# Short convolution of a hybrid decoder layer: taps on overlapping pieces of the product in PSUM, half of the tokens as one split tile with a halo, Silu in half 0

## Chip, cores and metric

The kernel runs on one core of a Trainium2 chip. The metric is the device time of one execution in microseconds (us). A core has TensorE (PE; its weight loads are listed as PEld), VectorE (DVE), ScalarE (ACT), GpSimd (POOL), and SyncE (SP), which issues the DMAs here.

## The reference, cut to what matters

One inference step of a two-layer decoder trunk, for a prompt of 2048 tokens and for a sample group of 8 single tokens with a cache of 2048 positions each. Layer 0 is a pooling mixer beside differential attention. Layer 1 is a gated DeltaNet beside a spatial-gating MLP. The change touches the front of layer 1, where the q, k and v channels (2304 of them) pass a causal convolution of four taps along the tokens and a Silu:

```python
qkv, u_sg, v_sg, b, a, gate = split_cols(h @ w_in, (CONV_CH, SG_W, SG_W, DELTA_HEADS, DELTA_HEADS, MIX_W))
ext = jnp.concatenate([conv_prefix.astype(qkv.dtype), qkv], axis=1)
conv = sum(ext[:, j:j + L] * conv_w[j] for j in range(CONV_WIDTH))       # CONV_WIDTH = 4
q, k, v = split_cols(jax.nn.silu(conv), (DELTA_W, DELTA_W, DELTA_W))     # DELTA_W = 768
q = l2norm(q.reshape(B, L, DELTA_HEADS, DELTA_DK)) * (DELTA_DK ** -0.5)
k = l2norm(k.reshape(B, L, DELTA_HEADS, DELTA_DK))
...
o, s_new = gated_delta_rule(q, k, v, beta, logg, s0)
...
return mixed @ w_out, ext[:, -(CONV_WIDTH - 1):], s_new, vv.reshape(B, L, SG_W)
```

The last three rows of `ext` are an output, `new_conv_prompt`.

## The kernel before

All products are done in three passes: each operand is split into a high and a low part of the type F32R (`hi`, `lo`), and `mm3` (lines 184 to 186) issues hi x hi, hi x lo and lo x hi into one PSUM bank. `fm_block` runs this over the eight slices of the 1024 model channels, 24 matmuls with 128 output channels on the partitions and the tokens as columns.

The stages follow one another: `in_even`, `attention`, `out_even` (layer 0's output product, the norm of layer 1 and the transposed, split tokens), then `odd` (layer 1). `odd` handles the 2048 tokens as two halves of 1024. The split tokens of a half lie in three pairs of tiles, of 512, 256 and 256 columns (`QSUB`), made by `h_subs` and `big_pair`. `out_even` fills those of half 0; the tokens of half 1 wait in DRAM (`hb`), and `load_half` loads and splits them when half 1 begins, with the 8 sample tokens as extra columns of the last pair.

For each half `odd` goes through 18 blocks of 128 convolution channels (`conv_silu`), with `gated_v` (the MLP's v part) and `decay` before block 14, and then through the spatial part and the gate blocks. In `conv_silu` each of the three subtiles gives one PSUM bank (`bank("acc")`, three banks in turn, tags X twice and D). ScalarE copies it into `raw` (line 1211), an SBUF tile with four columns ahead for the tokens before (`chalo`, lines 1206 and 1217). When a block's 1024 columns are in `raw`, two pieces of 512 follow: ScalarE multiplies by the first tap (line 1225), VectorE adds the other three in place (line 1227), ScalarE takes Tanh of half of it (line 1229), and VectorE makes (tanh + 1) * x (line 1230), which is twice the Silu; the constants of the delta stage (`delta_blocks`) take this factor into account. `store` writes the result to DRAM (`y1`), from where the delta stage reads it. `cx` and `cth` come from four buffers of 512 columns (`t512`).

Side work is interleaved by `tick`. In half 0 this is `sample_values`: for 8 sample rows, 16 pages of the value cache each are loaded by SP (line 531, three buffers `kp`), multiplied by GpSimd (line 626), added by VectorE (line 628), and summed over the partitions by TensorE (line 634). A page load is placed on SP behind the last `store` traced before it (`issue_after(self.mark)`). In half 1 it is the chunked delta rule of half 0 (`delta`), with a higher priority. The gate function `silu2_store` uses the same Tanh form (lines 418 and 420), with the second input read from PSUM. Weights are loaded and split one unit ahead (`w_unit`, lines 162 to 165).

The order of each engine's instructions is fixed when the kernel is built: a planner takes the traced order, the priorities and simulated ready times (`schedule_with_timeline_sim=True`). Each engine then runs its list in order.

Of the kernel before, what the change touches and what calls it, by code (L numbers as in the profile page):

```python
# [10 lines left out]
F32 = mybir.dt.float32  # L11
F32R = mybir.dt.float32r
BF16 = mybir.dt.bfloat16
I32 = mybir.dt.int32
AF = mybir.ActivationFunctionType
ALU = mybir.AluOpType
# [4 lines left out]
P = 128  # L21
D = 1024
NT = 2048
NS = 8
# [7 lines left out]
KT = 8  # L32
SUB = ((0, 384), (384, 384), (768, 256))
QSUB = ((0, 512), (512, 256), (768, 256))


# [25 lines left out]
class Net:  # L62
# [842 lines left out]
    def out_even(self):  # L905
        nc, I = self.nc, self.I
        st = ExitStack()
        self.bigs, self.t5 = {"b": 1, "s": 2}, T5
        self.banks = dict(acc="XXDA", h="Y", side="C")
        self.wp = self.pool(self.oddst, "wp", 2)  # L910
        self.wbufs = 2, 2, 1
        self.hp = hp = self.pool(self.oddst, "hp", 3)
        self.big = self.pool(self.oddst, "big", 1)
        wk = self.pool(st, "wk", 2, side="right")
# [7 lines left out]
        self.sides["values"] = self.sample_values()  # L922
        self.subs = self.h_subs(0, 0)
        for n, t in enumerate(P3):
# [9 lines left out]
            self.tick(VA if n < 8 else VB, "values")  # L934
        st.close()


    def odd_consts(self, st):
# [41 lines left out]
        nc.sync.dma_start(self.bmask, I["bmask"])  # L980
        self.chalo = t("chalo", [P, 18, 4])
        nc.gpsimd.memset(self.chalo, 0.0)
        self.S = [t(f"S{g}", [P, 3, P]) for g in range(2)]
# [73 lines left out]
    def odd(self):  # L1057
# [12 lines left out]
        for half in range(2):  # L1070
# [11 lines left out]
            for cb in range(18):  # L1082
                if cb == CB:
                    ba = self.gated_v(half, subs, wk, hp)
                    gt = self.decay(half, ba, wk)
                self.conv_silu(half, cb, subs, nxt(), wk, hp)
            if half == 0:
# [25 lines left out]
        self.tick(10000, "sample")  # L1113
        tiles = [self.big_pair(i, w) for i, (_, w) in enumerate(QSUB)]
        self.sides["w_out"] = self.w_out(I["w_out_o"], tiles, lambda: hp.tile([P, 4 + HALF], F32, tag="hx", name="wraw"), W2)
# [28 lines left out]
    def load_half(self, hp, wk):  # L1144

        nc = self.nc
        subs = self.h_subs(1, NS)
        for t in range(8):
            raw = hp.tile([P, 4 + HALF], F32, tag="hx", name="hk")[:, :D]
            nc.sync.dma_start(raw, self.hb[t])  # L1150
            raw = raw.rearrange("p (k t) -> p k t", t=P)
            hi, lo = self.tok_tile(subs, t)
            nc.scalar.copy(hi, raw)
            (nc.gpsimd if t % 3 == 2 else nc.vector).tensor_tensor(lo, raw, hi.bitcast(F32), ALU.subtract)
        hi, lo = (a[:, :, 256:] for a in subs[2][:2])
        nc.vector.tensor_copy(hi, self.hs)
        nc.vector.tensor_tensor(lo, self.hs, hi.bitcast(F32), ALU.subtract)
        return subs
# [42 lines left out]

    def conv_silu(self, half, cb, subs, unit, wk, hp):

        nc, O = self.nc, self.O
        raw = hp.tile([P, 4 + HALF], F32, tag="hx", name="raw")
        nc.vector.tensor_copy(raw[:, 0:4], self.chalo[:, cb, :])
        for hi, lo, t0, n, ns in subs:
            ps = self.bank("acc", 512)
            self.fm_block(ps[:, :n + ns], unit, (hi, lo))
            o = 4 + t0 - half * HALF  # L1210
            nc.scalar.copy(raw[:, o:o + n], ps[:, :n])  # L1211
            if ns:
                nc.vector.tensor_copy(self.raws[:, cb, :, 3], ps[:, n:n + ns])
            self.tick(self.pace)
            self.tick(2 if n == 512 else 1, "values")
        if half == 0:
            nc.vector.tensor_copy(self.chalo[:, cb, :], raw[:, HALF:HALF + 4])
        else:
            nc.sync.dma_start(O["new_conv_prompt"][cb * P:cb * P + P, :], raw[:, HALF + 1:HALF + 4],
                              allow_slow_non_contiguous=True)  # L1220
        w = self.convw[:, cb, :]
        for q in range(2):
            o = 1 + q * 512
            x = self.t512(wk, "cx")
            nc.scalar.mul(x, raw[:, o:o + 512], w[:, 0:1])  # L1225
            for j in range(1, 4):
                nc.vector.scalar_tensor_tensor(x, raw[:, o + j:o + j + 512], w[:, j:j + 1], x, ALU.mult, ALU.add)  # L1227
            th = self.t512(wk, "cth")
            nc.scalar.activation(th, x, AF.Tanh, scale=0.5)
            nc.vector.scalar_tensor_tensor(th, th, 1.0, x, ALU.add, ALU.mult)  # L1230
            c0 = half * HALF + q * 512
            self.store(self.y1[cb * P:cb * P + P, c0:c0 + 512], th)

# [113 lines left out]
    def delta_blocks(self, y, gt, dl):  # L1347
# [8 lines left out]
        s, c = (dl.tile([P, NH], F32, tag=nm, name=nm, bufs=3) for nm in ("ks", "kc"))  # L1356
        nc.vector.tensor_scalar(s, ss, 4 * EPS, 0.5, ALU.add, ALU.mult)
        self.rstd(ss, 4 * EPS)
        nc.vector.tensor_tensor(s, s, ss, ALU.mult)
        nc.vector.tensor_tensor(c, ss, ss, ALU.mult)  # L1360
        nc.vector.tensor_tensor(c, c, gt[0][:, y["t"], :], ALU.mult)

        nc.vector.tensor_scalar(qe, qe, P * EPS, 4 * P * EPS * EPS, ALU.mult, ALU.add)
        self.de(1).tensor_tensor(N, N, c[:, :, None].broadcast_to([P, NH, P]), ALU.mult)
# [395 lines left out]
```

## Time and profile before

| | |
|---|---|
| median of 3 runs | 3147.14 us (3144.58 to 3152.71) |
| the profiled execution | 3144.06 us |
| its span, first to last instruction | 3142.4 us |
| mean granted clock of TensorE | 0.958 of full speed |
| busy share of the span | PE 89%, PEld 80%, DVE 69%, ACT 48%, POOL 54% |

A busy share is the part of the span in which an engine had an instruction of the program running. Matmuls overlap in the records, so the work of TensorE is better read from the distance of their starts. A group of instructions is given by line, engine, operation, out<-in, shapes and count, then busy us, mean ns of one, and the idle time of the engine just before them with what ended it. L1227 is line 1227 of the kernel.

### The profile page before, as it was taken

Reading aid. Unit: us, or ns where it says so; the run is one execution under the profiler, and the core shown is the slowest. Engines: PE = TensorE matmul, PEld = TensorE weight load, DVE = VectorE, ACT = ScalarE, POOL = GpSimd, SP = SyncE. Lnnn points to the kernel's source line nnn. Section 1 sums busy time; section 2 is a strip of 40 time slices with the busy share of each in tenths; the row PEclk is TensorE's granted clock in tenths of the full one; section 3 lists DMA queues with packets and bytes.
Section 4 is the critical chain, followed back from the end, with each engine's and each line's share of the span. In section 5 each row is a group of like instructions: output and inputs, shape, how many; then the busy total and the mean of one; then the engine's idle time right before and its main releaser. Section 6 shows DMA issues by size and latency. Waiting matters only on the chain. (4 is left out here: it accounts for less than half of the span.)

```text
span 3142.4 us, 57680 instructions
## 1 busy us (share of the span) xinstructions
PE 2812.4 (89%) x20425; PEld 2515.9 (80%) x20425; DVE 2170.1 (69%) x4012; ACT 1516.3 (48%) x4464; POOL 1688.4 (54%) x1220
## 2 busy tenths in 40 slices
PE   8999899989998899989888778999899988878999
PEld 7999799889777777778777667888788877767887
DVE  5465456464998899876669998658788575457562
ACT  6643245534877787752222223445554533344331
POOL 4566545571667776664665655455544244255541
PEclk9999899999999999999998889999999999979999
DMA  4567766556244423237765554435333233467543
GB/s 164 167 192 254 240 219 202 190 166 183 70 102 118 121 60 84 71 101 221 245 217 180 164 164 160 130 103 154 86 95 100 82 99 112 121 159 212 164 119 98
DMA packets 423149, 462.55 MB, mean 147 GB/s; under 512 B 84683, under 2 KB 324212, under 8 KB 422860
## 3 DMA queue, kind: packets, MB, share of 16 engines
q1 hardware_dynamic: 422860, 458.86, 49.5%
q8 instruction: 162, 2.65, 0.4%
q14 instruction: 127, 1.04, 0.1%
HBM read 332.41 MB, written 126.33 MB: 146 GB/s over the span
## 5 line engine op out<-in xcount | busy, mean ns | idle before, releaser
L184 PE MATMUL acc<-sh,whi 128*128 128x256 f32 (+2 forms) x1328 | 392.5, 296 | 7.4 <-ACT raw L1211 4.8
L186 PE MATMUL acc<-sh,wlo 128*128 128x256 f32 (+2 forms) x1328 | 389.6, 294 | 1.5 <-DVE wlo L165 1.2
L185 PE MATMUL acc<-sl,whi 128*128 128x256 f32 (+2 forms) x1328 | 389.6, 293 | 0.0
L184 PE MATMUL acc<-bh,whi 128*128 128x512 f32 (+2 forms) x904 | 347.4, 384 | 23.9 <-ACT raw L1211 11.2
L186 PE MATMUL acc<-bh,wlo 128*128 128x512 f32 (+2 forms) x904 | 348.5, 386 | 6.6 <-DVE wlo L165 4.1
L185 PE MATMUL acc<-bl,whi 128*128 128x512 f32 (+2 forms) x904 | 346.3, 383 | 1.9 <-DVE bl L873 1.9
L813 ACT ACTIVATE p<-sc,nb 128x512 f32<-128x512 f32 (+3 forms) x480 | 302.3, 642 | 74.0 <-DVE nb L812 63.1
L836 POOL TENSOR_TENSOR p<-p,cf 128x512 f32<-128x512 f32 (+3 forms) x240 | 236.8, 1005 | 182.4 <-DVE cf L832 46.0
L626 POOL TENSOR_TENSOR kp<-kp,at 128x768 f32<-128x768 f32 x120 | 210.9, 1766 | 171.1 <-DMA kp<-in_cache_v 151.9
L165 POOL TENSOR_TENSOR wlo<-wraw,whi 128x1024 fp32r<-128x1024 f32 (+1 forms) x90 | 221.3, 2463 | 127.4 <-ACT whi L163 127.2
L812 DVE TENSOR_REDUCE nb<-sc 128x1 f32<-128x512 f32 (+3 forms) x480 | 276.0, 598 | 17.5 <-PE sc L809 9.1
L184 PEld LDWEIGHTS acc<-sh,whi 128*128 128x128 f32 (+1 forms) x1328 | 260.3, 196 | 17.5 <-ACT raw L1211 6.0
L548 POOL TENSOR_TENSOR kp<-kp,qb 128x768 f32<-128x768 f32 x88 | 168.9, 1925 | 183.6 <-DMA kp<-in_cache_k 133.8
L185 PEld LDWEIGHTS acc<-sl,whi 128*128 128x128 f32 (+1 forms) x1328 | 260.5, 196 | 6.5 <-issue 2.8
L186 PEld LDWEIGHTS acc<-sh,wlo 128*128 128x128 f32 (+1 forms) x1328 | 259.9, 196 | 4.7 <-issue 1.5
L184 PE MATMUL acc<-whi,bh 128*128 128x256 f32 x864 | 249.6, 289 | 0.3 <-DVE th L416 0.3
L185 PE MATMUL acc<-wlo,bh 128*128 128x256 f32 x864 | 248.3, 288 | 0.5 <-POOL wlo L165 0.5
L186 PE MATMUL acc<-whi,bl 128*128 128x256 f32 x864 | 248.4, 288 | 0.0
L1227 DVE SCALAR_TENSOR_TENSOR cx<-raw,convw,cx 128x512 f32<-128x512 f32 x216 | 230.9, 1069 | 11.2 <-ACT cx L1225 8.7
L850 PE MATMUL pv<-v,pt 128*128 128x128 f32 x1632 | 218.7, 282 | 15.9 <-ACT pt L848 9.1
L808 PE MATMUL sc<-kh,q 128*128 128x512 f32 (+2 forms) x480 | 210.5, 439 | 24.4 <-ACT p L813 20.9
L850 PEld LDWEIGHTS pv<-v,pt 128*128 128x128 f32 x1632 | 202.2, 195 | 30.5 <-ACT junk L853 13.8
(443 smaller groups left out, 8344.6 us busy)
## 6 DMA issues: line engine op xcount, KB each, us to landing
kp<-in_cache_k SPq DMA_DIRECT2D x128, 384.0 KB
kp<-in_cache_v SPq DMA_DIRECT2D x128, 384.0 KB
wraw<-in_w_in_e SPq DMA_DIRECT2D x56, 512.0 KB
wraw<-in_w_in_o SPq DMA_DIRECT2D x56, 512.0 KB
mc<-cat SPq DMA_DIRECT2D x72, 256.0 KB
mg<-sg SPq DMA_DIRECT2D x72, 256.0 KB
y<-cth SPq DMA_DIRECT2D x72, 256.0 KB
kh<-kh SPq DMA_DIRECT2D x48, 256.0 KB
```

Source lines behind the costliest of these rows:

```text
L165: e.tensor_tensor(lo, raw, hi.bitcast(F32), ALU.subtract)
L184: mm(out, ah, bh, start=first, stop=False)
L185: mm(out, ah, bl, start=False, stop=False)
L186: mm(out, al, bh, start=False, stop=last)
L548: (nc.vector if j % 3 == 2 else nc.gpsimd).tensor_tensor(k, k, qb, ALU.mult)
L626: nc.gpsimd.tensor_tensor(h3(w), h3(v), self.at[:, b, j, :, None].broadcast_to([P, NH, P]), ALU.mult)
L808: mm(sc[:, :w], qc, kh[:, c, :w], start=True, stop=False)
L812: nc.vector.tensor_reduce(nb[:, c, j:j + 1], sc[:, :n], AX.X, ALU.max, negate=True)
L813: nc.scalar.activation(p[:, c, :n], sc[:, :n], AF.Exp, bias=nb[:, c, j:j + 1], accum_out=l[:, c, j:j + 1])
L836: nc.gpsimd.tensor_tensor(p[:, 1, :n], p[:, 1, :n], cf[:, 1, j:j + 1].broadcast_to([P, n]), ALU.mult)
L850: mm(pv, tt[:, t, :], kvt[j][2][:, t, :], start=j == 0 and t == 0, stop=j * 4 + t == nk - 1)
L1227: nc.vector.scalar_tensor_tensor(x, raw[:, o + j:o + j + 512], w[:, j:j + 1], x, ALU.mult, ALU.add)
```

## The change

All tokens of a half, with four columns ahead of them for the last tokens of the half before and eight behind for the sample tokens, lie in one pair of split tiles (`hh`, `hl`). The convolution's product is taken in three pieces of 342, 342 and 340 output tokens (`CSUB`), each with the four columns ahead of it, so that neighbouring pieces overlap and every tap of a piece reads its PSUM bank directly. `raw` and `chalo` are gone. Half 0 uses ScalarE's Silu; half 1 keeps Tanh, with the taps halved beforehand (`convh`). The result is the Silu itself and not its double, so the delta stage's constants lose their factor. The last conv rows are collected in `clast` and written by one DMA. The other users of the subtiles get slices of the new pair (`odd_subs`).

```diff
+CSUB = ((0, 342), (342, 342), (684, 340))
+HW = 4 + HALF + NS
...
     def out_even(self):
-        self.big = self.pool(self.oddst, "big", 1)
+        big = self.pool(self.oddst, "big", 1)
+        self.hh, self.hl = (big.tile([P, KT, HW], F32R, name=nm) for nm in ("bh", "bl"))
+        for a in (self.hh, self.hl):
+            nc.gpsimd.memset(a[:, :, 0:4].bitcast(F32), 0.0)
...
-        self.subs = self.h_subs(0, 0)
+        self.subs = self.odd_subs(0, 0)
...
+    def odd_subs(self, half, ns):
+        return [(*(a[:, :, 4 + t0:4 + t0 + n + (ns if t0 == 768 else 0)] for a in (self.hh, self.hl)),
+                 half * HALF + t0, n, ns if t0 == 768 else 0) for t0, n in QSUB]
...
     def odd_consts(self, st):
-        self.chalo = t("chalo", [P, 18, 4])
-        nc.gpsimd.memset(self.chalo, 0.0)
+        self.clast = t("clast", [P, 18, 3])
+        self.convh = t("convh", [P, 18, 4])
+        nc.vector.tensor_scalar(self.convh, self.convw, 0.5, None, ALU.mult)
...
     def odd(self):
-                self.conv_silu(half, cb, subs, nxt(), wk, hp)
+                self.conv_silu(half, cb, nxt(), wk)
+            if half:
+                nc.sync.dma_start(O["new_conv_prompt"].rearrange("(k p) j -> p k j", p=P), self.clast,
+                                  allow_slow_non_contiguous=True)
...
-        tiles = [self.big_pair(i, w) for i, (_, w) in enumerate(QSUB)]
+        tiles = [tuple(a[:, :, c0:c0 + w] for a in (self.hh, self.hl)) for c0, w in QSUB]
...
     def load_half(self, hp, wk):
-        subs = self.h_subs(1, NS)
+        subs = self.odd_subs(1, NS)
+        for a in (self.hh, self.hl):
+            nc.gpsimd.tensor_copy(a[:, :, 0:4], a[:, :, HALF:HALF + 4].bitcast(F32))
...
-    def conv_silu(self, half, cb, subs, unit, wk, hp):
-        nc, O = self.nc, self.O
-        raw = hp.tile([P, 4 + HALF], F32, tag="hx", name="raw")
-        nc.vector.tensor_copy(raw[:, 0:4], self.chalo[:, cb, :])
-        for hi, lo, t0, n, ns in subs:
+    def conv_silu(self, half, cb, unit, wk):
+        nc = self.nc
+        w = (self.convw, self.convh)[half][:, cb, :]
+        for a, n in CSUB:
+            ns = NS if half and a + n == HALF else 0
+            m = n + 4 + ns
             ps = self.bank("acc", 512)
-            self.fm_block(ps[:, :n + ns], unit, (hi, lo))
-            o = 4 + t0 - half * HALF
-            nc.scalar.copy(raw[:, o:o + n], ps[:, :n])
+            self.fm_block(ps[:, :m], unit, tuple(h[:, :, a:a + m] for h in (self.hh, self.hl)))
+            x = self.t512(wk, "cx")[:, :n]
+            nc.scalar.mul(x, ps[:, 1:1 + n], w[:, 0:1])
+            for j in range(1, 4):
+                nc.vector.scalar_tensor_tensor(x, ps[:, 1 + j:1 + j + n], w[:, j:j + 1], x, ALU.mult, ALU.add)
             if ns:
-                nc.vector.tensor_copy(self.raws[:, cb, :, 3], ps[:, n:n + ns])
+                nc.vector.tensor_copy(self.raws[:, cb, :, 3], ps[:, n + 4:m])
+                nc.vector.tensor_copy(self.clast[:, cb, :], ps[:, n + 1:n + 4])
+            if half == 0:
+                th = x
+                nc.scalar.activation(th, x, AF.Silu)
+            else:
+                th = self.t512(wk, "cth")[:, :n]
+                nc.scalar.activation(th, x, AF.Tanh)
+                nc.vector.scalar_tensor_tensor(th, th, 1.0, x, ALU.add, ALU.mult)
+            self.store(self.y1[cb * P:cb * P + P, half * HALF + a:half * HALF + a + n], th)
             self.tick(self.pace)
-            self.tick(2 if n == 512 else 1, "values")
...
+            self.tick(1 if a else 2, "values")
...
     def delta_blocks(self, y, gt, dl):
-        nc.vector.tensor_scalar(s, ss, 4 * EPS, 0.5, ALU.add, ALU.mult)
-        self.rstd(ss, 4 * EPS)
+        nc.vector.tensor_scalar(s, ss, EPS, None, ALU.add)
+        self.rstd(ss)
...
-        nc.vector.tensor_scalar(qe, qe, P * EPS, 4 * P * EPS * EPS, ALU.mult, ALU.add)
+        nc.vector.tensor_scalar(qe, qe, P * EPS, P * EPS * EPS, ALU.mult, ALU.add)
```

In the diff of `conv_silu`, the removed tail (halo, the output DMA and the loop over two pieces of 512) is left out; it stands in the function above.

## Rows read from the trace of the kernel before

**Rows 1.** The page: busy tenths of PE and DVE in 40 equal slices.
```profile
PE   8999899989998899989888778999899988878999
DVE  5465456464998899876669998658788575457562
```

**Rows 2.** Windows by stage: busy (count) of PE, PEld, DVE, ACT, POOL; PEclk, DMA.
```profile
1400.00:1640.00 240.00, 215.52 (x1323) 189.82 (x1322) 152.68 (x143) 61.68 (x119) 146.99 (x102) 0.96 0.74 229
1640.00:1962.00 322.00, 255.21 (x1474) 219.37 (x1473) 294.94 (x304) 102.61 (x201) 175.73 (x95) 0.89 0.54 170
...
2172.00:2550.00 378.00, 351.86 (x2856) 317.72 (x2855) 294.78 (x593) 203.42 (x613) 159.66 (x111) 0.98 0.35 93
```

**Rows 3.** Groups of instructions on DVE from 1640 to 1962 us.
```profile
L1227 DVE SCALAR_TENSOR_TENSOR cx<-raw,convw,cx 128x512 f32<-128x512 f32 x105 | 122.1, 1163 | 1.2
L628 DVE TENSOR_TENSOR sacc<-sacc,kp 128x768 f32<-128x768 f32 x75 | 94.6, 1261 | 4.9 <-POOL kp L626 3.4 <-POOL sacc L626 1.4
L1230 DVE SCALAR_TENSOR_TENSOR cth<-cth,cx 128x512 f32<-128x512 f32 x35 | 30.0, 857 | 7.0 <-ACT cth L1229 7.0
...
L1217 DVE COPY chalo<-raw 128x4 f32<-128x4 f32 x18 | 15.6, 869 | 2.2 <-ACT raw L1211 2.2
L1206 DVE COPY raw<-chalo 128x4 f32<-128x4 f32 x17 | 13.2, 779 | 2.1 <-PE h L145 1.8
```

**Rows 4.** Groups of instructions on DVE from 2172 to 2550 us.
```profile
L1227 DVE SCALAR_TENSOR_TENSOR cx<-raw,convw,cx 128x512 f32<-128x512 f32 x105 | 101.9, 970 | 9.9 <-ACT cx L1225 8.7
L1230 DVE SCALAR_TENSOR_TENSOR cth<-cth,cx 128x512 f32<-128x512 f32 x35 | 28.0, 800 | 8.2 <-ACT cth L1229 7.9
```

**Rows 5.** Waits from 1640 to 1962 us: us in total, times, longest us.
```profile
ACT cth L1229 <- DVE cx L1227: 172.9, 35, 9.7
POOL kp L626 <- DMA kp<-in_cache_v: 86.4, 38, 9.6
...
PE side L634 <- DVE sacc L628: 24.5, 4, 7.7
...
PE acc L184 <- ACT raw L1211: 14.6, 5, 6.7
```

**Rows 6.** Timeline of PE, matmuls of 256 columns: start us, us.
```profile
1794.79 0.28 PE L184 MATMUL acc<-sh,whi 128*128 128x256 f32 x1
...
1795.02 0.28 PE L186 MATMUL acc<-sh,wlo 128*128 128x256 f32 x1
```

**Rows 7.** The same for 512 columns (three starts lie between the two).
```profile
1772.75 0.39 PE L185 MATMUL acc<-bl,whi 128*128 128x512 f32 x1
...
1773.67 0.39 PE L186 MATMUL acc<-bh,wlo 128*128 128x512 f32 x1
```

**Rows 8.** The same for 384 columns, in layer 0 (five starts between).
```profile
159.69 0.33 PE L186 MATMUL acc<-bh,wlo 128*128 128x384 f32 x1
...
160.73 0.33 PE L186 MATMUL acc<-bh,wlo 128*128 128x384 f32 x1
```

**Rows 9.** Groups by shape on DVE from 2000 to 2140 us: the gate blocks.
```profile
L420 DVE SCALAR_TENSOR_TENSOR th<-th,acc 128x256 f32<-128x256 f32 x12 | 4.9, 412 | 1.7 <-ACT th L418 1.7
...
L420 DVE SCALAR_TENSOR_TENSOR th<-th,acc 128x512 f32<-128x512 f32 x6 | 4.1, 678 | 2.2 <-ACT th L418 2.2
```

**Rows 10.** Groups by shape on PE from 1640 to 1962 us.
```profile
L634 PE MATMUL side<-sacc,ones 128*1 128x384 f32 x22 | 11.4, 606 | 24.5 <-DVE sacc L628 24.5
```

**Rows 11.** Timeline of SP's queue: issue us, us.
```profile
1710.32 0.36 SPq L531 DMA_DIRECT2D kp<-in_cache_v  x1
```

**Rows 12.** Timeline of POOL around the start of a row of pages.
```profile
1708.83 1.84 POOL L626 TENSOR_TENSOR kp<-kp,at 128x768 f32<-128x768 f32 x1 [9.63 <-DMA kp<-in_cache_v]
...
1713.43 1.47 POOL L626 TENSOR_TENSOR kp<-kp,at 128x768 f32<-128x768 f32 x1 [0.88 <-DMA kp<-in_cache_v]
```

**Rows 13.** Groups by shape on ACT: a load of a function table.
```profile
L1229 ACT ACT_TABLE_LOAD x1 | 1.3, 1283 | 0.0
```

**Rows 14.** Waits from 2172 to 2550 us: us in total, times, longest us.
```profile
ACT cth L1229 <- DVE cx L1227: 74.8, 27, 6.5
```

More of the change, by code (lines that the diff above doesn't have):

```diff
@@ L907, in out_even @@
         st = ExitStack()
-        self.bigs, self.t5 = {"b": 1, "s": 2}, T5
+        self.t5 = T5
         self.banks = dict(acc="XXDA", h="Y", side="C")
@@ L1200, in gate_block @@
         self.tick(self.pace)
-    def conv_silu(self, half, cb, subs, unit, wk, hp):
-        nc, O = self.nc, self.O
-        raw = hp.tile([P, 4 + HALF], F32, tag="hx", name="raw")
-        nc.vector.tensor_copy(raw[:, 0:4], self.chalo[:, cb, :])
-        for hi, lo, t0, n, ns in subs:
-            ps = self.bank("acc", 512)
-            self.fm_block(ps[:, :n + ns], unit, (hi, lo))
-            o = 4 + t0 - half * HALF
-            nc.scalar.copy(raw[:, o:o + n], ps[:, :n])
-            if ns:
-                nc.vector.tensor_copy(self.raws[:, cb, :, 3], ps[:, n:n + ns])
-            self.tick(self.pace)
-            self.tick(2 if n == 512 else 1, "values")
[L1216 to L1232, printed above, removed]
```

## Prediction

> **What bounds the kernel now.** I read the page first. TensorE is busy 89% of the span, so at first sight nothing but its own work could matter. The 40 slices say otherwise for one place: in the 22nd to the 25th, TensorE falls to 8, 7, 7, 8 tenths while VectorE stands at 9, 9, 9, 8 [rows 1]. That place is the convolution of half 0, and a table of windows by stage sizes it: between 1640 and 1962 us, 322 us long, VectorE is busy 294.9 us (92%), TensorE 255.2, GpSimd 175.7, ScalarE 102.6, at a mean granted clock of 0.89, so part of the time TensorE ran at 1.2 and not at 2.4 GHz. The stage before it has TensorE at 215.5 of 240 us with VectorE at 152.7, clock 0.96. The convolution of half 1 (378 us) has TensorE at 351.9 and VectorE at 294.8 [rows 2]. So half 0's stage is set by VectorE, half 1's by TensorE.
>
> Then VectorE's lines of that stage: the taps (L1227), their last step (L1230) and the two four-column copies (L1217, L1206) take 122.1 + 30.0 + 15.6 + 13.2 = 180.9 of the 294.9 us; the next is the sample group's page sums (L628), 94.6 us [rows 3]. One tap takes 1163 ns here and 970 in half 1, at the same shape [rows 3, 4]. Last the waits of the stage: ScalarE's Tanh waited 172.9 us for the taps, TensorE's sum over a row of pages 24.5 us for VectorE's page sum, and TensorE 14.6 us for `raw` copies that stood behind that Tanh on ScalarE [rows 5]. The sample pages run a chain of their own: DMA of a page into one of three buffers, GpSimd multiply, VectorE add.
>
> **TensorE's work does not change.** The pitch is the distance of starts: 0.115 us for 256 columns, 0.23 for 512, 0.173 for 384 [rows 6 to 8]. Before, an output block of 128 channels is 24 x (0.23 + 2 x 0.115) = 11.0 us. After, it is 72 matmuls of some 346 columns; between 256 and 384 the line gives 0.115 + 90/128 x 0.058 = 0.156, so 11.2 us. That is 36 x 0.2 = 7 us more in all at most, for the halo's 12 columns. If odd widths or starts at column 342 cost something, the nearest bound is the 384 pitch: 72 x 0.017 x 36 = 44 us more; the 0.45 ns per column that all three widths share gives no sign of it, and I take 0.
>
> **VectorE in half 0.** Removed: the 180.9 us above. Added: 18 x 9 taps of 342 columns whose first input is in PSUM. The trace has no such tap, but the same instruction with one input in PSUM: 412 ns at 256 columns, 678 at 512 [rows 9], so 146 ns + 1.04 ns per column, 502 ns at 342, and 162 x 0.502 = 81 us. The other end is the taps' own stretched rate, 342/512 x 1163 = 777 ns, 126 us. I take 502: rows 9 are the same form, and GpSimd worked there too. The Trainium skill (SBUF — State Buffer, Who interferes with whom) says that a VectorE instruction with two SBUF inputs contends with a GpSimd instruction that reads SBUF, and that one with at most one SBUF input does not. The trace agrees as far as 1163 against 970 ns for one shape can show it; by that rule the taps are 81 us, without it 126. Silu leaves the last step out. VectorE's work falls to 294.9 - 180.9 + 81 = 195 us (240 with stretched taps). It no longer bounds the stage.
>
> **What is late next in half 0.** TensorE's own work: 18 x 11.2 = 202 us, gated_v's 192 matmuls of 268 columns at 0.12 = 23, the sums over rows of pages at most 11 [rows 10]: 236 us. So of today's 322 us 67 are idle (322 - 255.2) and 19 the lower clock and small waits. The page chain: 80 pages in five rows of 16, which fill some 310 of the 322 us today, 62 us a row. From issue to GpSimd a page takes 3.1 us (1710.32 to 1713.43), then 1.5 to 1.8 us on GpSimd and 1.26 on VectorE, together some 6.2 us over three buffers, 2.1 us a page; with the gap of 9.6 us between two rows of pages that is 43 us a row, 215 for five [rows 3, 11, 12]. Three floors (VectorE 195, pages 215, TensorE 236) lie so close that no stage with a fixed order reaches them. I take the share of the stage before it, where no engine is full: 215.5/240 = 90% [rows 2]. 236/0.9 = 262 us, a gain of 60. The ends: all of it to 236 us, gain 86; or only the two TensorE waits above go, 24.5 + 14.6 = 39 us.
>
> **Half 1.** Removed: 101.9 + 28.0 us [rows 4] and some 5 us of copies. Added: 81 us of taps, 54 last steps with both inputs in SBUF at 342/512 x 800 = 534 ns, 29 us, and 18 more copies, 3 us. VectorE gains some 22 us, but TensorE sets this stage, with 26 us idle of 378. A fifth to a half of that, 5 to 13 us, is what a less loaded VectorE can give back; against it stands the bank wait below. I take 0.
>
> **ScalarE, SP and the rest.** The copies to `raw` go; three scaled copies and three activations of 342 columns take the place of two and two of 512, so ScalarE stays near 100 of 322 us, and of the rest it waited 172.9 us for taps [rows 5]. Silu may need another function table: a load is 1.28 us [rows 13]; a handful around gated_v and the decay, where Exp and Ln stand between Silus, is under 8 us, hidden by that slack; with no slack, 8 us once. Stores grow from 36 to 54 a half, at some 0.36 us of SP an issue [rows 11] 6 us a half; 18 small output DMAs become one. What is queued behind a store on SP are the page loads, now traced behind their own block's store: they wait for that block's Silu as they waited for the previous block's last step. The two halo copies on GpSimd, the memset, the halved weights and the merged hi/lo tiles I cost at nothing: they lie where the halves meet, under the last gate blocks and delta work of half 0; uncovered, 2 us once. In the delta stage only constants change.
>
> **Sum.** Against the profiled execution's own 3144.06 us, 3.1 below the median of the runs shown: 3144 - 60 + 0 = 3084 us.
>
> **Rivals.**
> - *The page chain sets half 0.* For it: GpSimd waits 86.4 us for pages [rows 5], and a row of pages takes 62 us. Against: its loads wait for buffers that VectorE frees late. If a row only falls to 58 or 60 us, the stage is 300 to 310, a gain of 12 to 22: 3122 to 3132.
> - *Slower: the taps hold the PSUM bank.* Today a block's bank is free after one ScalarE copy; then, after the scaled copy and three taps, behind whatever stands in VectorE's in-order queue. In half 1 that is the delta chain, which has priority: Tanh waited 27 times for taps there, up to 6.5 us [rows 14]. There are three banks, so two blocks of 24 x 0.156 = 3.75 us cover 7.5 us. It decides only where that lag passes 7.5 us so often that half 1's 54 blocks lose 60/54 = 1.1 us each. At 2 us each: 3144 - 60 + 108 = 3192. Against: VectorE has less to do in both halves.
> - *The change does not do what it says.* The planner lays each engine's order anew, and the late page sums and weight splits that stop TensorE may stop it elsewhere for as long: 3144, within 9 us.
>
> **How the numbers follow.** Forecast, gains of 25 to 100 us: 0.60. Page chain: 0.20, a quarter of it within 0.3%. No change: 0.08. Slower: 0.12. A measurement of this kernel tells from no change what is over some 0.3%, 9 us. Faster 0.60 + 0.15 = 0.75, same 0.05 + 0.08 = 0.13, slower 0.12. The range goes from 86 us in half 0 with 13 in half 1 (3045) to the slow end of the page chain with 3 us over it (3135); the last two cases are left out.
>
> **What would show it.** In the profile after: taps near 502 ns and none stretched; VectorE under 220 us in half 0's stage and the stage near 262 us; its granted clock over 0.93; matmuls of 346 columns at a pitch of 0.156; half 1's stage within 12 us of 378. The prediction is wrong if taps take over 650 ns, if the pitch nears 0.173, if a row of pages still takes 60 us, or if TensorE waits tens of us in half 1 for a bank, with `cx` as releaser.

## The result and the profile after

The changed kernel takes 3101.56 us (median of 4 runs, 3097.32 to 3109.30) against 3146.17 us for the kernel before on the same chip (4 runs, 3144.58 to 3152.71): ratio 0.9857, 95% interval 0.9838 to 0.9876, some 45 us less. The forecast was 3084 us, faster, with a range of 3045 to 3135. The profiled execution took 3097.32 us, its span is 3095.6.

On the page of the changed kernel, in the 40 slices, the dent in TensorE at the 22nd to 25th slice [rows 1] is shallower, and VectorE no longer stands at 9 there:

```profile
PE   8999899999998898989898888999999899858999
DVE  5465555564898999885677877567787574347662
```

Windows by stage of the changed kernel (columns as in rows 2): the stage before, the convolution of half 0, that of half 1.

```profile
1400.00:1632.00 232.00, 210.66 (x1298) 185.69 (x1299) 156.94 (x141) 59.94 (x116) 142.28 (x98) 0.96 0.73 233
1634.00:1920.00 286.00, 250.49 (x1489) 234.09 (x1489) 221.13 (x290) 94.68 (x185) 166.76 (x97) 0.96 0.63 190
2132.00:2513.00 381.00, 355.26 (x2823) 339.01 (x2822) 279.74 (x671) 186.44 (x587) 144.76 (x111) 0.97 0.31 93
```

Half 0's stage is 286 us where it was 322, VectorE is busy 221 us of it instead of 295, and the granted clock is 0.96 instead of 0.89. Half 1's stage is 3 us longer.

Groups of instructions on VectorE in half 0's stage of the changed kernel (they answer to rows 3), and then those of half 1 (rows 4):

```profile
L630 DVE TENSOR_TENSOR sacc<-sacc,kp 128x768 f32<-128x768 f32 x75 | 105.3, 1404 | 31.0 <-POOL kp L628 23.2 <-POOL sacc L628 6.1 <-PE acc L188 1.4
L1232 DVE SCALAR_TENSOR_TENSOR cx<-acc,convw,cx 128x342 f32<-128x342 f32 x108 | 60.7, 568 | 15.8 <-ACT cx L1230 13.4 <-DMA kp<-in_cache_v 1.0
L1232 DVE SCALAR_TENSOR_TENSOR cx<-acc,convw,cx 128x340 f32<-128x340 f32 x51 | 28.8, 564 | 8.4 <-ACT cx L1230 7.9
...
L1232 DVE SCALAR_TENSOR_TENSOR cx<-acc,convh,cx 128x342 f32<-128x342 f32 x108 | 61.5, 570 | 10.5 <-ACT cx L1230 9.0
...
L1242 DVE SCALAR_TENSOR_TENSOR cth<-cth,cx 128x342 f32<-128x342 f32 x36 | 26.7, 743 | 10.3 <-ACT cth L1241 10.1
```

A tap takes 568 ns beside the pages and 570 in half 1; the old ones took 1163 and 970. The page sums grew from 1261 to 1404 ns. And VectorE now waits for GpSimd's page product, 23.2 us in place of 3.4.

Waits of half 0's stage in the changed kernel (us in total, times, longest; they answer to rows 5), then the one of half 1 that a rival was about:

```profile
ACT cx L1238 <- DVE cx L1232: 116.7, 46, 8.5
POOL kp L628 <- DMA kp<-in_cache_v: 67.5, 34, 12.6
...
PE acc L186 <- DVE cx L1232: 28.4, 17, 5.4
DVE sacc L630 <- POOL kp L628: 23.2, 25, 2.2
...
PE side L636 <- DVE sacc L630: 2.7, 3, 1.5
...
PE acc L186 <- DVE cx L1232: 2.9, 1, 2.9
```

Of TensorE's two waits of rows 5 the one for `raw` (14.6 us) is gone and the one for the page sums fell from 24.5 to 2.7 us; in their place it waits 28.4 us for a PSUM bank that the taps still hold, in half 0, and 2.9 us in half 1.

The stages of all kernels of this study, each from the first to the last scaled copy of a half's convolution in its profiled execution (so a few us off the windows above); "rest" is the stretch from the end of half 1's convolution to the end of the span:

| kernel | median us | half 0 | VectorE, TensorE busy in it | half 1 | rest |
|---|---|---|---|---|---|
| before | 3146 | 320.1 | 294.5, 253.3 | 374.4 | 592.4 |
| changed | 3101.56 | 284.4 | 219.8, 248.9 | 377.1 | 583.7 |
| changed, banks7 | 3095.34 | 287.2 | 223.3, 246.0 | 392.4 | 573.2 |
| changed, sbuf_taps | 3164.48 | 324.2 | 266.3, 256.1 | 391.5 | 604.5 |
| changed, tanh0 | 3144.97 | 319.3 | 262.4, 261.5 | 376.6 | 597.0 |
| changed, nopages_after | 3040.06 | 241.2 | 122.7, 238.0 | 361.6 | 575.2 |
| before, nopages_before | 3055.11 | 229.0 | 155.5, 228.3 | 364.0 | 594.7 |
| before, silu_before | 3133.63 | 306.2 | 271.3, 246.7 | 372.7 | 596.5 |
| changed, prevmark | 3095.39 | 287.9 | 220.0, 247.2 | 366.0 | 586.4 |
| changed, pagefirst | 3094.73 | 290.4 | 227.9, 248.8 | 386.6 | 568.4 |
| changed, kx3 | 3118.97 | 293.5 | 223.2, 252.9 | 374.6 | 601.5 |
| changed, kx3_prev | 3126.90 | 300.7 | 228.9, 251.5 | 377.5 | 599.2 |
| before, kx3_before | 3154.87 | 324.4 | 296.6, 258.8 | 376.6 | 595.1 |
| changed, late_sums | 3064.21 | 253.7 | 217.9, 234.9 | 385.7 | 578.2 |

Of the 46.8 us between the two spans, 35.7 lie in half 0's stage and 8.7 in the rest; the stretch up to the first matmul of layer 0's output product, which the change does not touch, gave 6.3, the stretch from there to half 0's stage 1.4, and half 1 and the stretch between the halves took back 2.7 each. That first stretch took from 1385 to 1396 us in the 14 profiles, and half 1 and the rest differ by more than 10 us between kernels that do the same there: only the column of half 0 is read for causes below. It comes from one profiled execution a kernel, so its differences of a few us are not read either. Each experiment's ratio is to the kernel before on the same chip, whose medians there were 3145.8 to 3153.0 us.

### The profile page after: what moved, and what is told of

Same layout as the page of the kernel before. It is cut to its first block, busy times and chain, and to the rows that moved or that the text cites. A ratio compares the mean times of both kernels' runs of the same rounds, so it can differ in the third digit from the quotient of the medians.

```text
span 3095.6 us, 57877 instructions
## 1 busy us (share of the span) xinstructions
PE 2800.3 (90%) x20425; PEld 2541.6 (82%) x20425; DVE 2073.9 (67%) x4067; ACT 1492.5 (48%) x4431; POOL 1663.1 (54%) x1223
## 5 line engine op out<-in xcount | busy, mean ns | idle before, releaser
L186 PE MATMUL acc<-bh,whi 128*128 128x346 f32 (+6 forms) x2072 | 689.7, 333 | 42.0 <-DVE cx L1232 32.2
L188 PE MATMUL acc<-bh,wlo 128*128 128x346 f32 (+6 forms) x2072 | 687.3, 332 | 8.8 <-DVE wlo L167 8.2
L187 PE MATMUL acc<-bl,whi 128*128 128x346 f32 (+6 forms) x2072 | 686.3, 331 | 0.0
L186 PEld LDWEIGHTS acc<-bh,whi 128*128 128x128 f32 x2072 | 396.9, 192 | 64.8 <-issue 40.8
L188 PEld LDWEIGHTS acc<-bh,wlo 128*128 128x128 f32 x2072 | 396.4, 191 | 28.3 <-DVE wlo L167 10.2
L187 PEld LDWEIGHTS acc<-bl,whi 128*128 128x128 f32 x2072 | 397.0, 192 | 16.6 <-issue 3.1
L630 DVE TENSOR_TENSOR sacc<-sacc,kp 128x768 f32<-128x768 f32 x120 | 180.2, 1502 | 83.7 <-POOL kp L628 71.5
L165 ACT CAST whi<-wraw 128x1024 fp32r<-128x1024 f32 (+1 forms) x124 | 129.9, 1048 | 142.9 <-DMA wraw<-in_w_in_e 50.3
L841 DVE SCALAR_TENSOR_TENSOR p<-p,cf 128x512 f32<-128x512 f32 (+3 forms) x180 | 190.6, 1062 | 7.3 <-POOL p L838 6.6
L551 DVE TENSOR_REDUCE sc<-kp 128x12 f32<-128x768 f32 x128 | 119.1, 946 | 96.4 <-POOL kp L550 95.8
```

What stands on the lines that cost most here:

```text
L186: mm(out, ah, bh, start=first, stop=False)
L187: mm(out, ah, bl, start=False, stop=False)
L188: mm(out, al, bh, start=False, stop=last)
L630: nc.vector.tensor_tensor(acc, acc, v, ALU.add)
L841: nc.vector.scalar_tensor_tensor(p[:, 0, :n], p[:, 0, :n], cf[:, 0, j:j + 1], p[:, 1, :n], ALU.mult, ALU.add)
```

## The experiments

**What holds the stage at 284 us?** Two theories stood against each other: the bank that the taps hold (TensorE's 28.4 us), and the chain of the sample pages (*The page chain sets half 0* among the rivals).

*banks7*: seven PSUM banks in place of three for the products of half 0.

```diff
+            self.banks["acc"] = OD["acc"] if half else "XXDYYAB"
             for cb in range(18):
```

> The changed kernel with seven PSUM banks instead of three for the convolution's product in half 0 (the banks of the delta stage are free there; half 1 as it was). In the changed kernel TensorE waited 28 us in half 0's stage (286 us from 1634 to 1920) for a bank held by taps. Bank theory: with three banks TensorE cannot run ahead of taps that stand behind page sums; with seven these waits go, the stage falls by 20 to 28 us, total some 3075 against 3100. Rival, page chain: five rows of 16 pages at 55 us set the stage (276 of 286 us); the bank waits go but TensorE waits elsewhere, or the conv ends early and the pages are worked off behind it; total within 6 us of the changed kernel.

Measured: 3095.34 us (3077.73 to 3106.73, 6 runs), ratio 0.9824 (0.9789 to 0.9858), against 0.9857 of the changed kernel with overlapping intervals. Half 0's stage did not shrink. The waits of that stage in this kernel:

```profile
POOL kp L628 <- DMA kp<-in_cache_v: 93.6, 42, 10.4
...
PE side L636 <- DVE sacc L630: 31.9, 5, 8.5
```

TensorE never waits for a bank any more, and waits as long at the next thing in its queue that needs VectorE: the sum over a finished row of pages. The bank was a symptom.

*nopages_after*: pages 1 to 15 of the last five sample rows are left out (their loads, products and sums).

```diff
             for j in range(NJ):
+                if b >= 3 and j:
+                    ...
+                    continue
                 v = self.page(self.sv, I["cache_v"], b, j)
```

> The changed kernel, leaving out the sample pages 1 to 15 of the last five rows (loads, GpSimd multiplies and VectorE sums; the sample output is not the reference's). Page theory: half 0's stage falls from 286 to 245 to 255 us, which is TensorE's own work of some 240 us, total 3060 to 3070. Rival, taps and banks set the stage by themselves: it stays above 275 us, total above 3085.

Measured: 3040.06 us, ratio 0.9652 (0.9619 to 0.9685), half 0's stage 241.2 us with TensorE busy 238.0, a little below the 245 to 255 expected. The pages cost 43 us of the 284; TensorE's own floor was put at 236.

*nopages_before*: the same in the kernel before.

> The kernel before, with pages 1 to 15 of the last five sample rows left out (75 page loads, multiplications and sums; the output is then wrong for those rows). If what the change relieved in half 0 is the competition of the convolution and the pages for VectorE, then without the pages TensorE sets this stage in both kernels: the 320 us of half 0's convolution fall to 240 to 260 and the whole to 3040 to 3070, within 30 us of the changed kernel without pages (3040). If the gain is VectorE's shorter convolution whatever else it does, or TensorE's finer blocks, the stage stays above 280 and the whole above 3085, 45 us or more above the changed kernel without pages.

Measured: 3055.11 us (3049.22 to 3060.64, 4 runs), ratio 0.9707 (0.9675 to 0.9740). Without the pages the kernel before is quicker in this stage than the changed one, 229.0 against 241.2 us; the pages cost it 91 us. So the change gains nothing by itself in half 0's stage: it loses 12 us, with TensorE busy 238.0 against 228.3 us, and it halves what the pages cost. Over the whole kernel the changed one is still 15 us shorter without the pages; the table puts this into the rest (594.7 and 575.2 us), and why is open. Windows of half 0's stage, and VectorE's taps in it, first of the kernel before without pages, then of the changed one:

```profile
1640.00:1869.00 229.00, 228.31 (x1453) 200.91 (x1452) 155.49 (x234) 106.45 (x197) 40.80 (x23) 0.99 0.31 106
...
L1231 DVE SCALAR_TENSOR_TENSOR cx<-raw,convw,cx 128x512 f32<-128x512 f32 x105 | 79.1, 753 | 14.3 <-ACT cx L1229 11.9
```

```profile
1639.00:1880.00 241.00, 237.81 (x1493) 226.12 (x1492) 122.74 (x225) 102.45 (x202) 44.11 (x33) 1.00 0.37 114
...
L1236 DVE SCALAR_TENSOR_TENSOR cx<-acc,convw,cx 128x342 f32<-128x342 f32 x108 | 61.5, 573 | 51.2 <-ACT cx L1234 48.9
```

The old tap, both of its long inputs in SBUF, takes 753 ns where GpSimd multiplies almost no pages and 1163 where it does; the new one, with one of them in PSUM, 573 and 568. The Trainium skill (SBUF — State Buffer, Who interferes with whom) states that a VectorE instruction with two SBUF inputs contends with a GpSimd instruction that reads SBUF, and that one with at most one SBUF input does not; these four means agree.

**Which edit brings it?** *sbuf_taps* keeps everything but copies the product to SBUF first and lets the taps read the copy.

```diff
+            raw = self.hp.tile([P, 4 + HALF], F32, tag="hx", name="raw")[:, :n + 4]
+            nc.scalar.copy(raw, ps[:, :n + 4])
...
-                nc.vector.scalar_tensor_tensor(x, ps[:, 1 + j:1 + j + n], w[:, j:j + 1], x, ALU.mult, ALU.add)
+                nc.vector.scalar_tensor_tensor(x, raw[:, 1 + j:1 + j + n], w[:, j:j + 1], x, ALU.mult, ALU.add)
```

> The changed kernel, but ScalarE first copies each piece with its halo from PSUM to SBUF and the taps read the copy, as before the change; tiles, pieces, Silu stay changed. Contention theory (taps with two SBUF inputs lose time to GpSimd): taps in half 0 go from 567 ns to some 750, with no fixed value, VectorE in half 0's stage from 221 to some 250 us, stage 286 us or longer, total 3100 to 3120. Bank theory: the bank is free after one copy of about 0.45 us, the 28 us of bank waits go and outweigh the slower taps; stage some 265 us, total near 3080.

Measured: 3164.48 us (3155.31 to 3172.94, 10 runs), ratio 1.0051 (1.0027 to 1.0074): slower than before, 63 us over the changed kernel and well beyond both expected cases. 40 of the 63 us lie in half 0's stage. The edit also gives ScalarE 54 more copies a half. The taps take 827 and 1095 ns on VectorE in half 0:

```profile
L1234 DVE SCALAR_TENSOR_TENSOR cx<-raw,convw,cx 128x342 f32<-128x342 f32 x102 | 83.5, 827 | 13.5 <-ACT cx L1232 12.4
L1234 DVE SCALAR_TENSOR_TENSOR cx<-raw,convw,cx 128x340 f32<-128x340 f32 x48 | 52.5, 1095 | 4.6 <-ACT cx L1232 4.1
```

The Trainium skill (VectorE: DVE Perf Modes, Rules for kernel authors) says of elementwise work on a matmul's output to accept the 1x mode from PSUM, or to copy it to SBUF first where many operations follow. With three taps, beside GpSimd's page products, the measurement decides for PSUM.

*tanh0* gives half 0 the Tanh and last step of half 1.

```diff
-            if half == 0:
-                th = x
-                nc.scalar.activation(th, x, AF.Silu)
-            else:
```

> The changed kernel with half 0 done as half 1: Tanh and VectorE's last step instead of Silu, taps halved. VectorE gets 54 steps of some 0.65 us, 35 us, on top of 221 of 286 us in half 0's stage. Theory that VectorE's share still sets the pace through its queue: stage 10 to 25 us longer, total 3110 to 3125. Rival, VectorE has 65 us of idle time there and hides it: total within 6 us of the changed kernel, so that Silu brought nothing.

Measured: 3144.97 us (3135.94 to 3154.27, 10 runs), ratio 0.9983 (0.9965 to 1.0002): the whole gain is gone, more than either case expected, and half 0's stage is back at 319.3 us. The window of that stage and the group of last steps:

```profile
1639.00:1958.00 319.00, 261.25 (x1493) 244.59 (x1493) 262.52 (x348) 90.05 (x184) 165.20 (x99) 0.92 0.56 170
...
L1238 DVE SCALAR_TENSOR_TENSOR cth<-cth,cx 128x342 f32<-128x342 f32 x35 | 37.6, 1075 | 14.2 <-ACT cth L1237 14.1
```

VectorE is idle 56 of these 319 us, TensorE 58. So VectorE's share alone does not set the stage: 262 us busy give 319 here, and 295 gave 320 before the change.

*silu_before*: Silu in half 0 alone, in the kernel before.

```diff
+            if half == 0:
+                th = x
+                nc.scalar.activation(th, x, AF.Silu)
```

> The kernel before with Silu in half 0 alone (no last multiplication on VectorE there, in the query and key norms the constants that belong to it); the taps still read the copy in SBUF. It takes 30 us of VectorE out of half 0. If each edit pays by the VectorE time that it takes out, 3115 to 3125. If Silu pays only together with taps from PSUM (as Tanh in half 0 of the changed kernel took its whole gain), 3140 to 3150. If the short step behind the taps shortens the way to the store behind which the next pages are asked for, 3100 to 3115.

Measured: 3133.63 us (3120.60 to 3148.25, 10 runs), ratio 0.9963 (0.9943 to 0.9983), half 0's stage 306.2 us in the profiled execution, the fastest of the ten; the median lies between the first two cases. Silu alone is worth some 13 us, taps from PSUM alone (tanh0) 2, which is within the noise, both 45. The gains do not add up: each alone leaves a long last step or long taps in the way to the next store. For the last step this shows in the waits of SP's queue: the stores waited 88.1 us for it in tanh0 (41 times, 7.4 us the longest), and 42.1 us for Silu in the changed kernel (next part).

```profile
SPq L538 <- DVE cth L1238: 88.1, 41, 7.4
```

**Where does the chain of pages lose its time?** In this part a piece is one of the 54 pieces of 342 or 340 columns of a half, the work between two stores; the recorded expectations below call it a block. Means over the pages of half 0 in the changed kernel's trace, from one step's end to the next one's start: 2.3 us from a free page buffer to the load's issue, 4.2 until GpSimd begins, 1.7 for the product, 0.8 until VectorE begins, 1.4 for the sum: 10.4 us a round, three buffers, 3.4 us a page. In the kernel before, the wait of product for sum alone is 2.8 us and a page takes 3.9. What SP's queue waited for in half 0's stage, page loads for a page sum and stores for the last step or Silu, first in the kernel before, then in the changed one:

```profile
SPq L531 <- DVE sacc L628: 76.2, 45, 4.9
SPq L536 <- DVE cth L1230: 54.8, 29, 8.1
```

```profile
SPq L533 <- DVE sacc L630: 46.8, 37, 3.0
SPq L538 <- ACT cx L1238: 42.1, 30, 5.3
```

So about half of the loads go out as soon as a sum frees their buffer, and the others later, where SP comes to them. A stretch of the changed kernel's timeline (start us, us; idle time before and its releaser in brackets) shows a round:

```profile
1704.02 1.99 DVE L630 TENSOR_TENSOR sacc<-sacc,kp 128x768 f32<-128x768 f32 x1
1704.17 0.33 SPq L538 DMA_DIRECT2D y<-cx  x1
...
1706.04 0.33 SPq L533 DMA_DIRECT2D kp<-in_cache_v  x1
...
1709.62 1.65 POOL L628 TENSOR_TENSOR kp<-kp,at 128x768 f32<-128x768 f32 x1 [1.85 <-DMA kp<-in_cache_v]
1709.85 0.57 DVE L1232 SCALAR_TENSOR_TENSOR cx<-acc,convw,cx 128x342 f32<-128x342 f32 x1
1711.30 0.96 DVE L630 TENSOR_TENSOR sacc<-sacc,kp 128x768 f32<-128x768 f32 x1 [0.88 <-POOL kp L628]
1712.18 1.65 DVE L1232 SCALAR_TENSOR_TENSOR cx<-acc,convw,cx 128x342 f32<-128x342 f32 x3
...
1712.78 0.49 ACT L1238 ACTIVATE cx<-cx 128x342 f32<-128x342 f32 x1 [3.58 <-DVE cx L1232]
...
1713.29 0.33 SPq L538 DMA_DIRECT2D y<-cx  x1
```

The store at 1704.17 is out, and the page load behind it goes out at 1706.04, when the sum that began at 1704.02 has freed its buffer. GpSimd waits for that page, VectorE waits for GpSimd, the last tap of a piece stands behind that sum, Silu waits 3.58 us for the tap, and that piece's store, the second after the one at 1704.17, goes out at 1713.29. Three things could be loosened: the store ahead of the load, the number of buffers, and the place of the sum.

*prevmark* lets the page loads stand behind the store of the piece before.

```diff
-        self.mark = self.nc.sync.dma_start(dst, src).ins
+        self.prev, self.mark = getattr(self, "mark", None), self.nc.sync.dma_start(dst, src).ins
...
-        with self.tc.issue_after(self.mark):
+        with self.tc.issue_after(self.prev if cache is self.I["cache_v"] else self.mark):
```

> The changed kernel, but each load of a value page stands behind the store of the block before, not behind that of its own block. Nothing else is changed. If the stage of half 0 is set by a loop (store of the block, then page load, page product, page sum, which stands before the next block's taps), its 284 us fall to 250 to 270 and the whole to 3070 to 3090. If the three page buffers or the engines themselves pace the pages, the loads only wait elsewhere: 280 to 290 and 3092 to 3106. If earlier loads make GpSimd disturb VectorE more, 3106 to 3120.

*pagefirst* asks for the pages ahead of the piece's own store.

```diff
+            self.tick(1 if a else 2, "values")
             self.store(self.y1[cb * P:cb * P + P, half * HALF + a:half * HALF + a + n], th)
             self.tick(self.pace)
-            self.tick(1 if a else 2, "values")
```

> The changed kernel with the pages asked for ahead of the block's store in the program, so that SP issues them first and the store stands behind them; both the loads and the store are the same. If the wait for the block's own store paces the pages, 250 to 270 us for half 0's convolution and 3070 to 3090 in all, as with the loads behind the store of the block before. If buffers pace them, 3092 to 3106. If a load that waits for its page buffer then holds the block's store and with it the buffers of the convolution, the stage gets longer than 290 and the whole longer than 3106.

Measured: 3095.39 us (ratio 0.9835, 0.9809 to 0.9862) and 3094.73 us (0.9837, 0.9813 to 0.9860), half 0's stage 287.9 and 290.4 us. Loosening the store alone does nothing, which is the case expected if buffers or engines pace the pages.

*kx3* gives the pages six buffers while half 0's convolution runs.

```diff
+        if kx and j % 2:
+            t = kx.tile([P, 768], F32, tag="kx", name="kx", bufs=3)
+        else:
+            t = pool.tile([P, 768], F32, tag="kp", name="kp", bufs=3)
```

> The changed kernel with six page buffers in place of three while the half's convolution runs (every other page of the value cache goes into a second ring of three). If the three buffers pace the pages (a buffer's round takes 10.4 us in the changed kernel: 2.3 from free to the next load's issue, 4.2 until GpSimd begins, 1.7 for the product, 0.8 and 1.3 for the wait and the sum; a third of it is 3.45 us a page, and the stage moves 80 pages in 284 us), half 0's convolution falls from 284 to 245 to 265 us, towards TensorE's 241, and the whole to 3060 to 3085. If the order of the work on VectorE (a page's sum stands ahead of the next block's taps) or the banks that the taps hold set it, nothing moves: 3090 to 3106. If pages that come faster only disturb VectorE more, 3100 to 3115.

*kx3_prev* is that together with prevmark, *kx3_before* the six buffers in the kernel before.

> Six page buffers and the loads behind the store of the block before, both together. Alone the second did nothing (3095). If the store of the own block becomes the next limit once there are buffers enough, this is faster than six buffers alone, by 5 to 15 us: 3050 to 3075. If buffers were not the limit either, 3090 to 3106. If six buffers alone reach TensorE's bound, both come out alike.

> The kernel before with the same six page buffers. If the buffers paced the pages here too (a round of 11.8 us, a third of it 3.9 us a page), its half 0 falls from 320 us to VectorE's busy 295 or a little above, and the whole from 3147 to 3120 to 3135: the change then gained through the shorter wait between a page's product and its sum. If VectorE set the stage of the kernel before outright, it stays at 310 to 320 and 3140 to 3150.

Measured: 3118.97 us (3117.03 to 3122.30, 5 runs; ratio 0.9900, 0.9882 to 0.9917), 3126.90 us (0.9915, 0.9897 to 0.9933) and 3154.87 us (1.0009, 0.9995 to 1.0023). Half 0's stage is 293.5, 300.7 and 324.4 us: the theory that the buffers alone pace the stage fell too, in both kernels. kx3 and kx3_prev are even slower than the changed kernel (0.9900 and 0.9915 against 0.9857, the intervals apart), in the stage and in the rest; no case expected as much, and why is open. Waits of that stage with six buffers, and below them those of SP's queue:

```profile
POOL kx L632 <- DMA kx<-in_cache_v: 47.1, 12, 10.8
PE acc L186 <- DVE cx L1237: 31.1, 12, 5.0
POOL kp L632 <- DMA kp<-in_cache_v: 22.7, 11, 6.2
```

```profile
SPq L542 <- ACT cx L1243: 70.7, 31, 6.8
...
SPq L537 <- DVE sacc L634: 4.8, 7, 1.6
```

GpSimd waits for pages 69.8 us in sum, 67.5 in the changed kernel. The loads hardly wait for sums any more (4.8 us), but the stores, behind which they stand, wait longer for Silu (70.7 us): the wait moved along the round. What these edits had moved little shows in the order in which the instructions of the built kernels stand in the queues. Counted for the pages of half 0: how many pieces' taps have begun on VectorE ahead of a page's sum, beyond the last store ahead of its load on SP (the number of pieces, then how many pages have it).

```
changed     0: 7   1: 8   2: 30  3: 24  4: 1   5: 1
prevmark    0: 7   1: 7   2: 27  3: 24  4: 2
kx3         0: 6   1: 4   2: 21  3: 28  4: 10  5: 2
late_sums   0: 1   1: 3   2: 1   3: 2   4: 9   5: 28  6: 23
```

The planner lays most sums two or three pieces behind the load, with six buffers two to four. In the changed kernel the way from the load's issue to the sum's end is 4.2 + 1.7 + 0.8 + 1.4 = 8.1 us, plus a store and its Silu, against 4.5 us a piece of TensorE's (241/54). That two pieces, 9 us, just fail to cover it, so that each late page is passed on to the next store, is an argument from these means; no run shows it by itself.

*late_sums*: nine buffers, the load behind the store of the piece before, and the sum of a page bound behind the taps that are under way six pages later. It also gives the running sum of a row two tiles in place of one, and the sum over a row needs no page buffer any more.

```diff
+            def finish(acc, v, b, j): ...
+                with self.tc.issue_after(tm) if tm is not None else nullcontext():
+                    nc.vector.tensor_tensor(acc, acc, v, ALU.add)
...
+                late.append((acc, v, b, j))
+                while len(late) > (6 if kx else 0):
+                    finish(*late.pop(0))
...
+                self.tapmark = nc.vector.scalar_tensor_tensor(...).ins
```

> The changed kernel with nine page buffers, each load behind the store of the block before, and the sum of a page forced on VectorE behind the taps of the block that is under way six pages later. In the changed kernel, and in those with six buffers or an earlier load, the written order of the queues still puts a page's sum only two or three blocks of taps behind the store that its load follows on SP; a page takes about 10 us from there (0.6 to 2.3 until the issue, 4.2 until GpSimd begins, 1.7, 0.8, 1.3) and the next store about 3 more, against 5.3 us a block. Here the sum stands five to six blocks behind. If this loop through the queues, and not a resource, sets half 0's convolution, VectorE waits for GpSimd under 10 us in place of 25 to 36, TensorE's wait for the taps falls from 28 us to under 10, the stage from 284 to 245 to 262, and the whole to 3060 to 3085. If it is not the loop (transfers that come at their own rate, or VectorE and GpSimd in each other's way), the stage stays at 280 to 300 and the whole at 3090 to 3125, as with six buffers.

Measured: 3064.21 us (3059.44 to 3076.95, 6 runs), ratio 0.9740 (0.9709 to 0.9771), faster than both kernels: 37 us less than the changed one. Its window of half 0, three of its waits there, its page sums on VectorE and a stretch of its timeline:

```profile
1638.00:1892.00 254.00, 235.19 (x1445) 224.06 (x1446) 217.87 (x285) 92.23 (x184) 161.53 (x93) 0.97 0.66 205
```

```profile
POOL kx L641 <- DMA kx<-in_cache_v: 35.2, 13, 6.3
...
POOL kp L641 <- DMA kp<-in_cache_v: 13.6, 11, 2.5
...
PE acc L186 <- DVE cx L1241: 10.5, 5, 7.0
```

```profile
L625 DVE TENSOR_TENSOR sacc<-sacc,kx 128x768 f32<-128x768 f32 x45 | 66.7, 1483 | 0.8
...
L625 DVE TENSOR_TENSOR sacc<-sacc,kp 128x768 f32<-128x768 f32 x26 | 37.1, 1429 | 1.0 <-POOL kp L641 0.3
```

```profile
1701.97 1.78 DVE L1241 SCALAR_TENSOR_TENSOR cx<-acc,convw,cx 128x342 f32<-128x342 f32 x3
...
1703.66 2.11 DVE L625 TENSOR_TENSOR sacc<-sacc,kp 128x768 f32<-128x768 f32 x1
...
1705.87 0.96 DVE L625 TENSOR_TENSOR sacc<-sacc,kx 128x768 f32<-128x768 f32 x1
1706.74 1.79 DVE L1241 SCALAR_TENSOR_TENSOR cx<-acc,convw,cx 128x342 f32<-128x342 f32 x3
```

VectorE is as busy as in the changed kernel (218 us); what went is the waiting. VectorE stood idle 1.8 us ahead of the page sums, where it was 31.0 us, and three taps run in one piece. TensorE waits 10.5 us for taps in place of 28.4. The stage is 253.7 us, 12.5 above the 241.2 without any pages. A few pages have their sums ahead of the stage here (71 sums lie in it, 75 in the changed kernel); prevmark and kx3_prev, with 72 and 71, show that this brings nothing by itself.

So with the round through the in-order queues loosened (load behind sum and store, sum behind load, tap behind sum, store behind tap), 31 of the 43 us went that the pages cost half 0's stage in the changed kernel. Since earlier loads and six buffers, alone and together, gave nothing, the place of the sum is the step that none of the other runs had loosened. That it is enough by itself is not shown: late_sums changes the place of the sum, the buffers (nine, not six), the loads and the tiles of the running sum together, and no run has the later sums alone, or nine buffers and two running sums without them.

## Why the prediction was right, point by point

The time came out inside the range, and the stage, the direction and the short taps were foreseen. The size was in part luck: half 0's stage alone gave 36 us, and 11 us came from places where the forecast had nothing. The mechanism was that of a rival as much as that of the forecast: the page chain still held the stage.

- *What bounds the kernel.* Half 0's stage gained and half 1's did not: right. "So half 0's stage is set by VectorE" was too simple. With VectorE at 262 of 319 us (tanh0) the stage was as long as with 295 of 320. Without pages the kernel before needs 229 us with VectorE at 155. Long taps and the last step cost time beside the pages and not through VectorE's share alone.
- *Taps.* 502 ns was the estimate, 568 and 564 were measured, so 162 taps take 92 us and not 81. That they would not be stretched, by the row and by the rule, was right: 554 to 576 ns in half 0.
- *VectorE under 220 us.* 219.8 between the scaled copies and 221.1 in the window, so at the bound, and 195 was forecast: 11 us more for the taps, 11 more for page sums that slowed from 1261 to 1404 ns.
- *TensorE's work does not change.* Two starts of 346 columns in the changed kernel, with one start between them:

```profile
1700.21 0.32 PE L187 MATMUL acc<-bl,whi 128*128 128x346 f32 x1
...
1700.53 0.32 PE L186 MATMUL acc<-bh,whi 128*128 128x346 f32 x1
```

  0.32/2 = 0.16; the median distance over half 0 is 0.159, against 0.156. A block is 72 x 0.159 = 11.4 us and not 11.2, 0.4 over the 11.0 of before: 15 us in both halves, not 7. By this pitch it is 7 of the 12 us between the stages without pages (229.0 and 241.2); half 1's window is 3 us longer (378 to 381), too little to read.
- *What is late next in half 0.* Here is the term that was mis-sized: 236/0.9 = 262 us. TensorE's floor came out at 241, near the 236, but the share at 241/284 = 0.85. The share was borrowed from the stage before, in which no convolution stands in the queues with the pages. The gain was 36 us and not 60, just under the lower end of 39 given for it. The floor of 215 us for the page chain was wrong in its parts: it took 3.1 us from issue to GpSimd from one page, the mean is 4.2, and it left out the 2.3 and 0.8 us of waits; measured, a page takes 3.4 us and not 2.1.
- *Half 1: 0.* 381 against 378 us, within the 12 us named. VectorE's load there fell from 295 to 280 us and gave nothing back.
- *ScalarE and tables: 0.* Five table loads stand in half 0's stage where three stood (1.28 us each); ScalarE is busy 95 of 286 us and waits 116.7 us for taps. No run priced them by themselves.
- *The rivals.* The page chain did hold half 0, with a row of 16 pages in 49 to 55 us and not in 62 or 43; it cost less than its rival said (stage 284, not 300 to 310). The bank wait came, but in half 0 and as a symptom; in half 1 it was 2.9 us. "It does not do what it says" fell.
- *The sum.* 3144 - 60 = 3084 was forecast. The stage gave 36, and 11 us net came from stretches that the change hardly touches. One profile of each kernel does not tell how much of this is scatter; the 8.7 us in the rest were not followed up.

## What to carry to other kernels

Where no engine is full and yet a stage is long, look for a closed round of in-order queues: here a sum placed close behind its load held taps, taps held stores, and sums and stores held the next loads. More banks, six buffers or an earlier issue did nothing here while the consumer kept its place in its queue; with more buffers and the consumer five to six pieces behind the load, in place of two to three, the kernel took 37 us less. In half 0's stage, taps that read the product in PSUM paid for their longer work on TensorE only beside GpSimd's page products (284 against 320 us with the pages, 241 against 229 without).

## What the runs showed of the hardware

- A tap of 342 or 340 columns with one input in PSUM and a weight per partition took 552 to 576 ns, with GpSimd busy 44 of 241 or 167 of 286 us of the stage; with both inputs in SBUF 512 columns took 753, 970 or 1163 ns in the mean, with GpSimd busy 41 of 229, 160 of 378 and 176 of 322 us.
- Reading the product where it lies or copying it first is 63 us apart in this kernel (3101.56 and 3164.48), 40 of them in half 0's stage.
- The granted clock of half 0's stage was lower where TensorE stood idle longer: 0.89 with 255 busy of 322 us, 0.92 with 261 of 319 (tanh0), 0.96 with 250 of 286, 0.97 with 235 of 254, 1.00 with 238 of 241. The idle time alone does not give it: banks7 had 0.92 with 247 of 288. What the clock gave late_sums is not shown apart from its waits.
